# A diffusion-transformer layer on one core: probabilities transposed in squares on VectorE by way of DRAM, partial sums copied back into PSUM, Newton rounds on GpSimd

## The chip, the core and the metric

The kernel runs on one core of one Trainium2 chip. The metric is device time in microseconds (us), the median of several executions. The engines are named TensorE (PE in the profile, its weight loads PEld), VectorE (DVE), ScalarE (ACT), GpSimd (POOL) and SyncE (SP), which here issues all DMAs. SBUF is the on-chip memory, PSUM the banks that TensorE writes. The page of the profile calls buffers by the program's names, with their numbers left out.

## The reference

One layer over 256 latent tokens and 256 context tokens, width 2048, all in fp32:

```python
sh1, sc1, g1, sh2, sc2, g2 = ada_mods(c, w_ada, b_ada)          # from the conditioning vector
qa, ka, va, qb, kb, vb = mixer_qkv(modulate(x, sh1, sc1), w_in, ...)      # 8+8 query heads, 2+2 key heads of 128
...                                                             # the same for the context tokens
heads = concat(window_sink_attention(qa, ka, va, context), global_attention(qb, kb, vb, context))
x = layer_norm(ALPHA * x + g1 * (heads @ w_out), ln1_g, ln1_b)
x = layer_norm(ALPHA * x + g2 * swiglu(modulate(x, sh2, sc2), w_gate, w_up, w_down), ln2_g, ln2_b)
```

Group A has rotary positions, a window and a sink logit per head; group B has RMS-normalised queries and keys (`rms_norm`) and rotary positions. Every latent query sees 256 latent and 256 context keys, so the probabilities of one head for 128 queries are a tile of 128 x 512.

## The kernel before, in words

**Precision.** An fp32 product is made of three passes: each operand is split into a rounded part (`hi`, a cast on ScalarE) and the rest (`lo`, a subtraction on VectorE), and `mm3` (L268 to L271) adds hi x hi, hi x lo and lo x hi in a PSUM bank. A weight piece of 128 x 1024 is cast in L491 and split in L494. Matmuls of plain fp32 (transposes, values) go without a split.

**The first half, up to the first layer norm,** is a list of steps. Each step has an engine, a cost in ns, steps that it must follow, buffers that it takes and gives back, and a due time (`F.at`). The class `Flow` (L67) walks through the list forward and backward in `ROUNDS` rounds, with the costs, the lags between engines (`SAME`, `OTHER`) and the pools, and keeps the order of the round that ends first. The instructions are then issued in that order, and each engine runs its own list strictly in order. So the cost numbers in `F.add` decide the order, not the speed. SyncE's list holds the loads of the weights (1 MB each, in four `raw` and two `araw` buffers) and all other DMAs.

- *Input projection.* The 16 slices of the width are taken in groups of 1, 1, 2, 4 and 8 (`GROUPS`, numbered g = 0 to 4). For each group, the modulated inputs are made (`flow_inputs`), then six blocks of 512 columns (`flow_block`, L646): four query blocks of two row tiles (latent tokens) and two key/value blocks of four row tiles (latent and context). Each row tile takes one of four `acc` banks. At the end of a group the bank is added to a sum in SBUF (`qacc`, `kvacc`) by VectorE (L679), or copied there in group 0.
- *Keys and queries* (`flow_keys`, `flow_queries`): the norm's 1/sqrt comes from squares on ScalarE (L715) and three Newton rounds on VectorE (L287 to L290, `rsqrt_steps`), then rotary multiplications on VectorE, transposes on TensorE, cast and split.
- *Attention* (`flow_attend`, L847): four head groups (gi = 0 to 3) with four pairs each; a pair is two heads for 128 queries, 16 pairs in all. A pair's steps are: scores for both heads (TensorE, banks of the pool `wk`), maximum (VectorE, L873), exponent (ScalarE, L885), inverse of the sum (VectorE), weighing (ScalarE, L898), transposes of the probabilities in four 128 x 128 tiles per head (TensorE, L903), gather of each head's transposed tile from PSUM into `pT` (ScalarE, L908), values (four fp32 matmuls of 256 columns, L914), cast and split of the result (L921, L925).
- *Output projection* (`flow_out`, L1042): per 512 columns, first over early head groups (`first_outs`), whose sums are kept in `outacc`, then over the last ones. VectorE adds bank and sum (L1086), multiplies by the gate (L1089), adds the residual (L1092) and takes statistics (L1098). For the last 512 columns (`by_tile`) the early sum is gated and added ahead (L1089, L1092), so that after the last matmul only the bank's own part is left (L1095).
- Beside this, VectorE sums adaLN vectors (`vector_sum`, L377), and idle time of TensorE at the start is filled with 56 matmuls on the identity (L1124).

**The second half** (FFN, both projections and the second layer norm) is not touched by the change. It transposes its hidden tiles with the way that the change brings to attention: VectorE turns each 32 x 32 square in place and reorders the squares (`squares`, L1367), four DMAs put the result to DRAM so that the rows land in transposed order (`put`, L1372), and one DMA gets it back (`get`, L1377).

Of the kernel before, what the change touches and what calls it, by code (L numbers as in the profile page):

```python
# [22 lines left out]
P = 128  # L23
# [12 lines left out]
NB = 512  # L36
# [17 lines left out]
PUT, GET, PLACE = 6, 8, 9  # L54

# [11 lines left out]
class Flow:  # L67
# [5 lines left out]
    SAME = {"SP": 0, "PE": 0, "ACT": 60, "DVE": 80, "POOL": 80}  # L73
    OTHER = {"SP": 2000, "PE": 270, "ACT": 90, "DVE": 90, "POOL": 150}
# [120 lines left out]
def dit_layer(ctx: ExitStack, tc: tile.TileContext, x, c, cx, c_ctx, w_ada, b_ada, w_in, q_norm_g,  # L195
# [72 lines left out]
    def mm3(ps, xh, xl, w, first, last):  # L268
        nc.tensor.matmul(ps, lhsT=xh, rhs=w[0], start=first, stop=False)  # L269
        nc.tensor.matmul(ps, lhsT=xh, rhs=w[1], start=False, stop=False)  # L270
        nc.tensor.matmul(ps, lhsT=xl, rhs=w[0], start=False, stop=last)  # L271

    def rsqrt_steps(ss, n, done):
# [12 lines left out]
        def newton(i):  # L286
            y, t = st["y"], st["t"]  # L287
            nc.vector.scalar_tensor_tensor(t, y, -0.5, y, op0=ALU.mult, op1=ALU.mult)
            nc.vector.tensor_mul(t, t, ss())
            nc.vector.scalar_tensor_tensor(y, t, 1.5, y, op0=ALU.add, op1=ALU.mult)  # L290
            if i == 2:
                done(y)

        return [first] + [lambda i=i: newton(i) for i in range(3)]

    ea = ExitStack()
# [203 lines left out]

    def flow_products(hl, deps, ready, cols, ps, xs, first, last, prev):

        def fn():
            if first:
                ps.t = acc_bank()
            for i, (c, x) in enumerate(zip(cols, xs)):
                xh, xl = x()
                mm3(ps.t, xh, xl, (hl.hi[:, c : c + NB], hl.lo[:, c : c + NB]),
                    first and i == 0, last and i == len(cols) - 1)
# [3 lines left out]
        return F.add("PE", 681 * len(cols), fn, after, [ps] if first else [], list(hl.rooms))  # L513
# [71 lines left out]
    def flow_part(k0, n, at, each):  # L585
# [17 lines left out]
        for s in range(2):  # L603
# [3 lines left out]
            for j0 in range(0, n, 2):  # L607
# [33 lines left out]
                b = F.add("DVE", 60 + 330 * nj, rest, [a], give=[uf])  # L641
# [4 lines left out]
    def flow_block(g, b, chunks):  # L646
# [7 lines left out]
        ends = {}  # L654
# [19 lines left out]
        for r in rows:  # L674
            dst = qacc[gi][r] if kvi is None else kvacc[kvi][r // 2][:, r % 2, :]

            def evac(dst=dst, ps=accs[r], r=r):
                if g > 0:
                    nc.vector.tensor_add(dst, dst, ps.t)  # L679
                elif r % 2 or b < 2:  # L680
                    nc.vector.tensor_copy(dst, ps.t)
                else:
                    nc.scalar.copy(dst, ps.t)

            eng = "ACT" if g == 0 and not (r % 2 or b < 2) else "DVE"
            evacs[b, r] = F.add(eng, 520 if eng == "ACT" else 710, evac, [ends[r], evacs.get((b, r))], give=[accs[r]])
# [19 lines left out]
    def head_rms(srcs, nh, after, scale=None):  # L706
# [10 lines left out]
        def done(y):  # L717
            if scale is not None:
                f = pa.tile([P, n], F32, tag="qsc", name="qsc", bufs=4)
                nc.vector.tensor_scalar_mul(f, y, scale)  # L720
# [899 lines left out]
```

## Time and profile before

| | |
|---|---|
| median of 3 runs | 1156.09 us (1155.67 to 1156.09) |
| the profiled execution | 1156.38 us, of which 1154.6 us are the span from the first to the last instruction |
| granted TensorE clock, mean | 0.996 |
| instructions in the span | 14326 |
| moved by DMA | 304.49 MB |
| first scores, first transpose after the output projection | at 214.25 us, at 406.15 us of the span |

How to read the lines: busy lines give us, share and count for each engine. A row of a stretch gives each engine's busy us and count, then the granted clock, the share of time that the 16 DMA engines were busy, and GB/s. A group's row is line, engine, operation, written<-read, shape and count, then busy us and mean ns of one, then the idle time just before and what ended it. A row of the chain of waits is start, us, engine, tile and line. A row of the order of time is start, us, engine, line and operation. A DMA row gives the count, KB of each and the median us from issue to landing. The durations of neighbouring instructions of one engine overlap in part.

### The profile page before, as it was taken

The numbers are of one execution on the slowest core, as the hardware profiler recorded it, in microseconds if no ns is written. First come the engines' busy times: TensorE is split into PE (matmuls) and PEld (weight loads), VectorE is DVE, ScalarE is ACT, GpSimd is POOL, SyncE is SP. The second block draws the span as 40 slices with busy tenths as digits, with TensorE's granted clock in tenths as the row PEclk, the third lists the DMA queues.
The fourth block names the chain that finished last, engine by engine and source line by source line (L and its number), as shares of the span: only waits on it lengthen the run. The fifth ranks groups of instructions, "written<-read, shape, count | busy, mean of one in ns | idle before, by whom it ended". The sixth has DMA issues, their size and how long they took to land.

```text
span 1154.6 us, 14326 instructions
## 1 busy us (share of the span) xinstructions
PE 1135.0 (98%) x5475; PEld 919.1 (80%) x5475; DVE 830.9 (72%) x1078; ACT 540.2 (47%) x772; POOL 26.1 (2%) x44
## 2 busy tenths in 40 slices
PE   8999999999999999999999999999999999999995
PEld 8766588888888768888888888888888888888884
DVE  4763489988899988777666666776776787676556
ACT  3331442678776255544464444544544344433341
POOL 1000030000000001000000000000000000000000
PEclk9999999999999999999999999999999999999998
DMA  8999998624588578989967776677677988876641
GB/s 263 382 381 394 396 363 311 221 74 160 185 316 296 175 250 309 349 305 317 312 196 258 224 244 223 225 248 250 227 247 248 323 308 301 315 292 236 208 142 74
DMA packets 166557, 304.49 MB, mean 264 GB/s; under 512 B 7340, under 2 KB 33356, under 8 KB 164183
## 3 DMA queue, kind: packets, MB, share of 16 engines
q1 hardware_dynamic: 166488, 303.58, 75.7%
q8 instruction: 43, 0.70, 0.2%
q14 instruction: 26, 0.21, 0.1%
HBM read 295.68 MB, written 7.86 MB: 263 GB/s over the span
## 4 chain that ended last, share of the span: by engine, by line
PE 94%; DVE 2%; DMA 2%; ACT 1%; issue 0%; SPq 0%; DVEq 0%; ACTq 0%
PE acc L269 27%; PE acc L270 27%; PE acc L271 27%; PE wk L914 2%; PE wk L530 2%; PE acc L1124 1%; PE wk L903 1%; DMA raw<-in_w_in_dram 1%; PE wk L269 1%; PE wk L271 1%; PE wk L270 1%; PE wk L387 1%; PE wk L617 1%; DMA lgb<-in_ln_b_dram 1%; PE wk L967 0%
## 5 line engine op out<-in xcount | busy, mean ns | idle before, releaser
L260 DVE TENSOR_TENSOR lo<-raw,hi 128x1024 fp32r<-128x1024 f32 x258 | 312.5, 1220 | 182.8 <-ACT hi L259 179.3
L259 ACT CAST hi<-raw 128x1024 fp32r<-128x1024 f32 x258 | 271.2, 1055 | 353.4 <-PE acc L271 306.5
L269 PE MATMUL acc<-hi,u2h 128*128 128x512 f32 x704 | 274.6, 390 | 0.2 <-ACT u2h L1443 0.2
L270 PE MATMUL acc<-lo,u2h 128*128 128x512 f32 x704 | 274.0, 389 | 0.7 <-DVE lo L260 0.7
L271 PE MATMUL acc<-hi,u2l 128*128 128x512 f32 x704 | 274.1, 389 | 0.0
L269 PEld LDWEIGHTS acc<-hi,u2h 128*128 128x128 f32 x704 | 132.2, 188 | 28.2 <-ACT u2h L1443 1.1
L270 PEld LDWEIGHTS acc<-lo,u2h 128*128 128x128 f32 x704 | 132.2, 188 | 28.2 <-DVE lo L260 1.1
L271 PEld LDWEIGHTS acc<-hi,u2l 128*128 128x128 f32 x704 | 132.2, 188 | 28.2 <-DVE u2l L1444 0.6
L491 ACT CAST hi<-raw 128x1024 fp32r<-128x1024 f32 (+1 forms) x86 | 87.9, 1033 | 127.2 <-PE acc L271 64.4
L269 PE MATMUL acc<-hi,hTh 128*128 128x512 f32 x344 | 135.5, 394 | 0.0
L271 PE MATMUL acc<-hi,hTl 128*128 128x512 f32 x344 | 133.9, 389 | 0.0
L270 PE MATMUL acc<-lo,hTh 128*128 128x512 f32 x344 | 133.9, 389 | 0.0
L377 DVE SCALAR_TENSOR_TENSOR adav<-raw,cs,adav 128x512 f32<-128x512 f32 (+1 forms) x128 | 121.2, 947 | 9.1 <-DMA raw<-in_w_ada_dram 7.4
L494 DVE TENSOR_TENSOR lo<-raw,hi 128x1024 fp32r<-128x1024 f32 (+1 forms) x86 | 101.8, 1195 | 27.2 <-ACT hi L491 27.0
L269 PE MATMUL acc<-hi,uh 128*128 128x512 f32 x256 | 103.9, 406 | 0.1
L270 PE MATMUL acc<-lo,uh 128*128 128x512 f32 x256 | 100.3, 392 | 0.8 <-DVE lo L494 0.8
L271 PE MATMUL acc<-hi,ul 128*128 128x512 f32 x256 | 100.0, 391 | 0.0
L270 PEld LDWEIGHTS acc<-lo,hTh 128*128 128x128 f32 x344 | 64.6, 188 | 14.4 <-issue 1.0
L269 PEld LDWEIGHTS acc<-hi,hTh 128*128 128x128 f32 x344 | 64.6, 188 | 14.1 <-issue 1.0
L271 PEld LDWEIGHTS acc<-hi,hTl 128*128 128x128 f32 x344 | 64.6, 188 | 13.4
L269 PEld LDWEIGHTS acc<-hi,uh 128*128 128x128 f32 x256 | 48.1, 188 | 15.8 <-issue 5.2
L270 PEld LDWEIGHTS acc<-lo,uh 128*128 128x128 f32 x256 | 48.2, 188 | 10.5 <-DVE lo L494 1.8
(206 smaller groups left out, 1167.5 us busy)
## 6 DMA issues: line engine op xcount, KB each, us to landing
raw<-in_w_ada_dram SPq DMA_DIRECT2D x72, 1024.0 KB, 7.3
raw<-in_w_gate_dram SPq DMA_DIRECT2D x44, 1024.0 KB, 7.3
raw<-in_w_up_dram SPq DMA_DIRECT2D x44, 1024.0 KB, 7.3
raw<-in_w_down_dram SPq DMA_DIRECT2D x44, 1024.0 KB, 5.2
raw<-in_w_ada_dram SPq DMA_DIRECT2D x48, 512.0 KB, 4.5
raw<-in_w_in_dram SPq DMA_DIRECT2D x18, 1024.0 KB, 9.9
raw<-in_w_out_dram SPq DMA_DIRECT2D x16, 1024.0 KB, 5.0
raw<-in_w_in_dram SPq DMA_DIRECT2D x10, 512.0 KB, 6.9
```

The lines of the kernel that those rows point to most:

```text
L259: nc.scalar.copy(hi[:, :n], raw[:, s : s + n])
L260: nc.vector.tensor_tensor(lo[:, :n], raw[:, s : s + n], hi[:, :n].bitcast(F32), op=ALU.subtract)
L269: nc.tensor.matmul(ps, lhsT=xh, rhs=w[0], start=first, stop=False)
L270: nc.tensor.matmul(ps, lhsT=xh, rhs=w[1], start=False, stop=False)
L271: nc.tensor.matmul(ps, lhsT=xl, rhs=w[0], start=False, stop=last)
L377: nc.vector.scalar_tensor_tensor(a[:, c : c + piece], raw[:, f : f + piece], cs[:, 4 * (g * (G4 * NB // w) + j) + 2, None], a[:, c : c + p ...
L387: nc.tensor.matmul(ps, lhsT=ones, rhs=sb[:, s : s + NB], start=True, stop=True)
L491: nc.scalar.copy(hl.hi[:, :n], raw.t[:, s : s + n])
L494: nc.vector.tensor_tensor(hl.lo[:, :n], raw.t[:, s : s + n], hl.hi[:, :n].bitcast(F32), op=ALU.subtract)
L530: nc.tensor.matmul(bank.t[32 * j : 32 * j + 32, :width], lhsT=cs[:, 4 * k + 2 - 2 * i : 4 * k + 34 - 2 * i], rhs=raw.t[:, c * width : (c + ...
L617: nc.tensor.transpose(ps.t[:, (j * 2 + t) * P : (j * 2 + t + 1) * P], src, ident)
L914: nc.tensor.matmul(o_ps.t[:, : 2 * P], lhsT=v, rhs=pT.t[:, k].rearrange("p h q -> p (h q)"), start=k == 0, stop=k == 3)
```

## The change

Three parts, and new costs for the planner:

1. *Probabilities.* Transposes (L903) and gathers (L908) are dropped. VectorE turns a head's 128 x 512 tile in 32 x 32 squares into `hx`; SyncE puts both heads of a pair to DRAM with four DMAs and gets `pT` back with one. The value matmuls now read their 256 columns as eight pieces of 32.
2. *Sums.* In the last group of the input projection (`SEED_G` = 4), and in the output projection where an earlier sum exists, ScalarE copies the sum from SBUF into the bank (`flow_seed`), and the matmuls add to it (no `start`). At the end ScalarE copies the bank out (or VectorE gates it at once). VectorE's adds are dropped there, and the early gating of the last 512 columns with them.
3. *Norms.* The Newton rounds of the head norms, and the scaling behind them, run on GpSimd: four operations a round instead of three, since the combined operation is not used there.
4. The planner's costs and lags are set to other values (examples below), a trip through DRAM is given `SLOW` = 1500 ns more per way, the filler at the start takes a bank of the pool `wk` instead of `acc`, and the DRAM pool is opened earlier.

```diff
+SEED_G = 4
+SLOW = 1500
...
-    SAME = {"SP": 0, "PE": 0, "ACT": 60, "DVE": 80, "POOL": 80}
-    OTHER = {"SP": 2000, "PE": 270, "ACT": 90, "DVE": 90, "POOL": 150}
+    SAME = {"SP": 0, "PE": 0, "ACT": 120, "DVE": 80, "POOL": 80}
+    OTHER = {"SP": 2000, "PE": 270, "ACT": 180, "DVE": 160, "POOL": 150}
...
-            nc.vector.scalar_tensor_tensor(t, y, -0.5, y, op0=ALU.mult, op1=ALU.mult)
-            nc.vector.tensor_mul(t, t, ss())
-            nc.vector.scalar_tensor_tensor(y, t, 1.5, y, op0=ALU.add, op1=ALU.mult)
+            nc.gpsimd.tensor_mul(t, y, y)
+            nc.gpsimd.tensor_mul(t, t, ss())
+            nc.gpsimd.tensor_scalar(t, t, -0.5, 1.5, op0=ALU.mult, op1=ALU.add)
+            nc.gpsimd.tensor_mul(y, y, t)
...
+    def flow_seed(ps, src, after):
+        def fn():
+            ps.t, ps.seeded = acc_bank(), True
+            nc.scalar.copy(ps.t, src())
+        return F.add("ACT", 475, fn, after, [ps])
...
+        ends = {r: flow_seed(accs[r], lambda r=r: sums[r], [evacs[b, r], chunks[0][0][1][0]]) for r in rows} if g >= SEED_G else {}
...
+            eng = "ACT" if g >= SEED_G or g == 0 and not (r % 2 or b < 2) else "DVE"
+            def evac(dst=sums[r], ps=accs[r], eng=eng):
+                if eng == "ACT":
+                    nc.scalar.copy(dst, ps.t)
+                elif g > 0:
                     nc.vector.tensor_add(dst, dst, ps.t)
...
-        for f in rsqrt_steps(lambda: st["ss"], n, done):
-            prev = [F.add("DVE", 720, f, prev)]
+        for i, f in enumerate(rsqrt_steps(lambda: st["ss"], n, done)):
+            prev = [F.add("POOL" if i else "DVE", 1300 if i else 720, f, prev)]
...
-            def flip(i, probs=probs, ps=None):
-                ps.t = wk_bank()
-                for k in range(4):
-                    nc.tensor.transpose(ps.t[:, k * P : (k + 1) * P], probs[i].t[:, k * P : (k + 1) * P], ident)
-            def gather(i, pT=pT, ps=None):
-                if i == 0:
-                    pT.t = b4([P, 4, 2, P], F32, "pT")
-                nc.scalar.copy(pT.t[:, :, i, :], ps.t.rearrange("p (k q) -> p k q", k=4))
+            def squares(i, probs=probs, hx=hx):
+                if i == 0:
+                    hx.t = b4([P, 2, NB], F32, "hx")
+                nc.vector.transpose(hx.t[:, i, :].rearrange("p (r k q) -> p k r q", r=4, k=4),
+                                    probs[i].t.rearrange("p (k r q) -> p k r q", r=4, k=4))
+            def put(hx=hx, st=st):
+                st["hd"] = scratch.tile([4, 32, 2, 4, P], F32, tag="pd", name="pd", bufs=8)
+                for a in range(4):
+                    nc.sync.dma_start(st["hd"][:, :, :, a, :].rearrange("r i h x -> i h r x"),
+                                      hx.t[32 * a : 32 * a + 32].rearrange("i h (r x) -> i h r x", r=4))
+            def get(pT=pT, st=st):
+                pT.t = b4([P, 2, 4, P], F32, "pT")
+                nc.sync.dma_start(pT.t.rearrange("p h a x -> p (h a x)"), st["hd"].rearrange("r i h a x -> (r i) (h a x)"))
...
+                pv = pT.t.rearrange("p h a (k q) -> p k (h a) q", k=4)
                 for k in range(4):
...
-                    nc.tensor.matmul(o_ps.t[:, : 2 * P], lhsT=v, rhs=pT.t[:, k].rearrange("p h q -> p (h q)"),
+                    nc.tensor.matmul(o_ps.t[:, : 2 * P].rearrange("p (g q) -> p g q", q=32), lhsT=v, rhs=pv[:, k],
                                      start=k == 0, stop=k == 3)
...
-            m = [F.add("DVE", 700, lambda i=i, f=largest: f(i), [s[i]]) for i in range(2)]
+            m = [F.add("DVE", 610, lambda i=i, f=largest: f(i), [s[i]]) for i in range(2)]
...
+                g.append(F.add("DVE", 615, lambda i=i, f=squares: f(i), [n[i], *g], [hx] if i == 0 else [], [probs[i]]))
+            a = F.add("SP", 1800, put, g, give=[hx])
+            g = [(F.add("SP", 1300, get, [(a, -SLOW)], [pT]), -SLOW)]
+            v = F.add("PE", 1760, values, g, [o_ps], [pT, *kv_room[w]])
...
+        ends = {t: flow_seed(accs[t], lambda t=t: outacc[n, t], [outs[n, t], first]) for t in range(NT)} if gs[0] else {}
...
-            elif by_tile:
-                at, F.at = F.at, F.at - 6
-                early = steps([outs[n, t], gates[n]], lambda: gate(lambda: outacc[n, t]), base)
-                F.at = at
-                outs[n, t] = steps([ends[t], early], lambda: gate(lambda: ps.t), last, spread, give=[ps])
...
+            a = F.add("DVE", 710, gate, [ends[t], gates[n]], give=[ps])
+            a = F.add("DVE", 710, base, [(a, 80)])
+            outs[n, t] = F.add("DVE", 710, spread, [(a, 80)])
```

More of the change, by code (lines that the diff above doesn't have):

```diff
@@ L508, in fn @@
                 mm3(ps.t, xh, xl, (hl.hi[:, c : c + NB], hl.lo[:, c : c + NB]),
-                    first and i == 0, last and i == len(cols) - 1)
+                    first and not seed and i == 0, last and i == len(cols) - 1, ps.seeded)
         after = [deps[0], (deps[1], 200), ready[0], (ready[1], 400), prev]
-        return F.add("PE", 681 * len(cols), fn, after, [ps] if first else [], list(hl.rooms))
+        return F.add("PE", 688 * len(cols), fn, after, [ps] if first and not seed else [], list(hl.rooms))
     last_load = []
@@ L653, in flow_block @@
         accs = [Buf("acc") for r in rows]
-        ends = {}
+        sums = [qacc[gi][r] if kvi is None else kvacc[kvi][r // 2][:, r % 2, :] for r in rows]
+        ends = {r: flow_seed(accs[r], lambda r=r: sums[r], [evacs[b, r], chunks[0][0][1][0]]) for r in rows} if g >= SEED_G else {}
         done = 0
```

90 lines of the change are left out of this document (34 added, 56 removed).

## The prediction

> **What bounds the kernel now.** I read first the page's busy line and its chain that ended last, then the table of stretches.
>
> ```profile
> PE 1135.0 (98%) x5475; PEld 919.1 (80%) x5475; DVE 830.9 (72%) x1078; ACT 540.2 (47%) x772; POOL 26.1 (2%) x44
> PE 94%; DVE 2%; DMA 2%; ACT 1%; issue 0%; SPq 0%; DVEq 0%; ACTq 0%
> ...
> core 0: us, PE busy (x) PEld busy (x) DVE busy (x) ACT busy (x) POOL busy (x), PEclk, DMA share, GB/s
> 0.00:200.00 200.00, 195.89 (x1193) 147.51 (x1194) 125.83 (x170) 70.50 (x105) 14.08 (x25) 1.00 0.98 356
> 200.00:406.00 206.00, 206.00 (x1020) 166.80 (x1018) 184.48 (x327) 133.26 (x275) 1.77 (x4) 1.00 0.59 204
> 440.00:1133.00 693.00, 692.27 (x3079) 572.60 (x3078) 474.09 (x499) 313.66 (x348) 9.26 (x14) 1.00 0.76 259
> ```
>
> The chain is TensorE for 94% of the span, at full granted clock. Up to 200 us it shares the bound with DMA (share 0.98). From 200 to 406 us, where attention and the output projection lie and where nearly the whole change acts, TensorE has no gap and DMA is busy only 0.59 of the time. After that the code is the same. So an instruction less on TensorE in the second stretch is worth its full time, as long as nothing else arrives later. VectorE is the nearest competitor (184.5 of 206 us). DMA is very unevenly used there:
>
> ```profile
> 240.00:260.00 20.00, 20.00 (x103) 15.91 (x102) 16.98 (x47) 14.67 (x43) 0.00 (x0) 1.00 0.33 106
> 320.00:340.00 20.00, 20.00 (x98) 16.77 (x98) 18.79 (x25) 13.41 (x27) 0.00 (x0) 1.00 0.90 316
> ```
>
> **The change part by part.** *1. TensorE loses the transposes of the probabilities.* In order of time, the chain shows a group of four and its neighbours:
>
> ```profile
> 223.00 0.44 PE wk L903 x4
> 358.73 0.87 PE wk L903 x8
> 357.00 1.73 PE wk L914 x8
> 359.60 0.23 PE acc L269
> L903 PE MATMUL wk<-ident,pr 128*128 128x128 f32 x128 | 18.4, 272 | 0.0
> ```
>
> The 272 ns of one overlap with its neighbours; the chain's 0.44 us for four is what the engine's stream is longer by. There are 128 / 4 = 32 groups: 32 x 0.44 = **14.1 us** off. The order of the changed program, from the first score matmul to the first transpose after the output projection, has the same 604 matmuls of 512 columns and 64 value matmuls (0.23 and 0.43 us), but 48 transposes where there were 176; TensorE gets nothing new.
>
> *2. In their place: VectorE squares, ScalarE loses the gathers, SyncE gains 80 DMAs.*
>
> ```profile
> L1367 DVE STREAM_TRANSPOSE spill<-spill 128x512 f32<-128x512 f32 x20 | 13.0, 685 | 0.0
> L908 ACT COPY pT<-wk 128x512 f32<-128x512 f32 x32 | 18.5, 595 | 4.4 <-PE wk L903 4.0
> L679 DVE TENSOR_TENSOR qacc<-qacc,acc 128x512 f32<-128x512 f32 x6 | 4.1, 680 | 0.6 <-PE acc L271 0.6
> L679 DVE TENSOR_TENSOR kvacc<-kvacc,acc 128x512 f32<-128x512 f32 x4 | 2.6, 681 | 0.5 <-PE acc L271 0.5
> L1086 DVE TENSOR_TENSOR oacc<-oacc,acc 128x512 f32<-128x512 f32 x8 | 5.4, 679 | 0.3 <-PE acc L271 0.2
> L1080 ACT COPY oacc<-acc 128x512 f32<-128x512 f32 x8 | 4.8, 595 | 1.3 <-PE acc L271 1.3
> L288 DVE SCALAR_TENSOR_TENSOR rs_t<-rs_y 128x8 f32<-128x8 f32 x9 | 1.4, 156 | 0.0
> 252.86 1.28 DVE L873 TENSOR_REDUCE m<-wk 128x1 f32<-128x512 f32 x2
> ```
>
> VectorE gains 32 x 0.685 = 21.9 us. It loses 16 adds of the last group of the input projection (10.9), 8 adds of the output projection (5.4), two early gates and two early adds (2.8), and 29 Newton instructions (29 x 0.156 = 4.5). The net is -1.7 us, but only ten of the 16 adds lay behind 200 us (the two L679 rows are of that stretch), so there it is about +2.4: 187 busy of 192 us. Durations overlap (two reductions take 1.28, not 1.37), so at the pace of 0.60 for 512 elements the stretch is some 90 to 94% full. ScalarE loses 32 gathers and gains 26 seeds and 18 copies out: +12 x 0.595 = 7.1 us on 133. Both stay under TensorE; I cost them at nothing. The seeds need cover: a bank's next use now waits for copy out and copy in (1.19 us) instead of one add (0.68). Behind a key/value block three other rows are still to run, 3 x 6 x 0.23 = 4.1 us, and a query block takes two of four banks. Without that cover 18 seeds in the input and output sums would cost up to 0.5 us each, 9 us.
>
> *3. The added wait: values wait for a trip through DRAM.* Each of the 16 pairs of heads now goes squares, four puts of 128 KB, one get of 512 KB, values. The nearest rows are the same trip at half size, in the FFN:
>
> ```profile
> hd<-spill SPq DMA_DIRECT2D x80, 64.0 KB, 4.3
> spill<-hd SPq DMA_DIRECT2D x20, 256.0 KB, 5.3
> L1372 SPq DMA_DIRECT2D hd<-hx x8: 430/438/660, 901.9 to 910.7; - x8
> DMA to landing us min/median/max: 1.6/4.5/7.1
> DMA to landing us min/median/max: 5.6/6.4/7.1
> raw<-in_w_ada_dram SPq DMA_DIRECT2D x12, 1024.0 KB, 5.0
> raw<-in_w_ada_dram SPq DMA_DIRECT2D x16, 512.0 KB, 4.5
> ```
>
> The first landing line is that of the tile hd (all its puts and gets), the second that of hx (eight puts at the busiest time); the last two rows are of the stretch from 200 to 406 us. The last put leaves 3 x 0.44 = 1.3 us after the first, lands 4.3 later, and the get takes 5.3: 10.9 us. For the doubled size I add 0.5, which is what 512 KB more cost the loads of this stretch: **11.4 us**. Below, two landings of 1.6 plus the issue make 4.5; above, 1.3 + 7.1 + 7.1 = 15.5.
>
> How long may it take? In the new order the tightest pair is the sixth. From its scores to its values TensorE has 63 matmuls of 512 (14.5), two other pairs' values (3.5) and eight transposes (0.9): 18.8 us. VectorE, in its order from that pair's last reduction to its second square, has three reductions and four squares (7 x 0.61), two splits of a weight piece (2 x 1.14), two half tiles (2 x 0.34) and six small ones (6 x 0.19): 8.4, with about 0.2 for the start. That leaves 10.2, and 9.8 when what VectorE is still behind with is carried along. The others, counted alike, have 10.2 to 15.7 (pairs 14, 15, 16: 10.2, 11.2, 10.7). A trip of 11.4 is late by 1.6 at pair 6; pairs 7 and 8 are under way and move along. It is late again by 1.2 at pair 14, which carries 15 and 16. **TensorE waits 2.8 us.** SyncE's queue is in order too: behind a put that waits for its squares stand weight loads. The order has one or two between the puts of two pairs, each load has one of four buffers, and up to 300 us DMA has room, so I cost this at nothing beyond the 2.8.
>
> From the ninth get to the sixteenth it has none: 13 loads of 1 MB, 28 puts and 7 gets, 21 MB, are in the queue between them, and TensorE's work between these values is 28 x 0.43 + 166 x 0.23 = 50 us. The most that DMA moves in this trace is
>
> ```profile
> 100.00:120.00 20.00, 20.00 (x104) 13.97 (x106) 6.58 (x9) 1.99 (x2) 0.00 (x0) 1.00 1.05 405
> ```
>
> so 21 MB want 52 us. I take this as inside the 1.2 at pair 14; it is the first place to look if I am wrong.
>
> *4. Newton rounds on GpSimd.* 36 dependent operations, between 279 and 944 ns each by the rows below, 12 per norm: 3.3 to 11.3 us. The first norm has 5 us of VectorE work between its start and its user; the others much more. Cost nothing; 6 us at worst.
>
> ```profile
> L960 POOL TENSOR_TENSOR mA<-lcol,sc 128x4 f32<-128x4 f32 x4 | 3.8, 944 | 286.7 <-DVE sc L975 286.7
> L962 POOL TENSOR_TENSOR mB<-mB,sh 128x4 f32<-128x4 f32 x4 | 1.1, 279 | 0.3
> ```
>
> *5. The order.* The planner's costs change too, and with them the lists of all engines. Ahead of the first scores TensorE's list has the same instructions, and SyncE's differs by a few exchanged loads. DMA is full there, and TensorE has one gap:
>
> ```profile
> 120.00:140.00 20.00, 19.15 (x119) 11.93 (x112) 8.65 (x12) 11.19 (x18) 0.00 (x0) 1.00 1.04 393
> ```
>
> An exchanged load of 1 MB can close that gap of 0.85 or open another like it. I take nothing, and 1 us to both sides.
>
> *Sum.* The profiled execution took 1156.38 us, 1154.6 of span and 1.8 around it: 1156.4 - 14.1 + 2.8 = 1145.1. It lies 0.3 above the median of the three runs, so I forecast **1144.8**.
>
> **The rivals.** *A. No wait at all: 1142.0.* Where DMA share is 0.33, as around pair 6, a landing is nearer the 1.6 than the 4.3; the trip is then 5 to 9 us, under every room. Against it speak pairs 14 to 16. The Trainium skill, page "DMA: Bandwidth & Descriptors", section "Anatomy of one DMA", has, for DMAs that GpSimd issues, 2.0 us fixed plus bytes at 436 GB/s: an estimated 8.1 us for this trip and so this case; no run before shows an idle trip, and the FFN's 4.3 and 5.3 are longer.
>
> *B. VectorE becomes the bound: about 1150.* If the 187 us are nearer to 97% than to 92% of 192, in-order waits of 5 us more are likely. GpSimd may add to it: while it built tables, two VectorE operations ran 0.36 and 0.12 us long.
>
> ```profile
> 163.69 1.64 DVE L377 SCALAR_TENSOR_TENSOR g1b<-raw,cs,g1b 128x1024 f32<-128x1024 f32 x1 [2.90 <-DMA raw<-in_w_ada_dram]
> 165.26 1.34 DVE L494 TENSOR_TENSOR lo<-raw,hi 128x1024 fp32r<-128x1024 f32 x1
> L377 DVE SCALAR_TENSOR_TENSOR g1b<-raw,cs,g1b 128x1024 f32<-128x1024 f32 x17 | 21.7, 1277 | 0.2 <-DMA raw<-in_w_ada_dram 0.2
> ```
>
> At half a microsecond for each of 38 operations a full block costs 19 us of VectorE, some 5 beyond its slack: 1150 again. The Trainium skill, page "SBUF — State Buffer", section "SBUF: two separate sides", has this as an exclusive lock on a shared port pair; by the row above the loss was partial.
>
> *C. The trip is late everywhere: 1162, slower.* At the FFN's busiest time puts land in 6.4; with 7.1 for the get the trip is 1.3 + 6.4 + 7.1 = 14.8. Scores to values is about 21 us of a stretch of 137, so lateness is paid about 6.5 times; 14.8 exceeds the rooms by 3 on average: 6.5 x 3 = 19.5, 1156.4 - 14.1 + 19.5 = 1161.8. It decides from 14.1 / 6.5 = 2.2 average lateness, a trip of about 14 us. For it: the 21 MB in 50 us. Against: the 5.0 that 1 MB loads take in this stretch.
>
> *D. Values get slower: up to 1170.* Their moving operand now comes in eight pieces of 32 columns. Doubled, 16 x 1.73 = 27.7 is lost; half as long again already eats the gain. No row has such a matmul; on VectorE, pieces of 32 cost what a plain tile costs:
>
> ```profile
> L741 DVE TENSOR_TENSOR qrot<-qacc,sinQ 128x256 f32<-128x256 f32 x4 | 1.7, 416 | 0.0
> L788 DVE TENSOR_TENSOR kTl<-wk,kTh 128x256 fp32r<-128x256 f32 x8 | 3.1, 416 | 1.7 <-ACT kTh L785 1.7
> ```
>
> **How the numbers follow.** Forecast (1142.5 to 1149) 60%; A 12%; B 10%; C 14%, of which 4 end within 0.2% of before; D 4%. 0.2%, 2.3 us, is about what a measurement of this kernel can tell from none. So faster 82%, same 4%, slower 14%. From 1141 to 1156 some 15% is left out above (C, D) and 5% below (the far side of A, and a start that gains from its new order).
>
> **What would show it.** Right: the values' group unchanged at 1.73 us; no transposes of probabilities on TensorE; the first transpose after the output projection near 395 us instead of 406; TensorE's waits in the stretch named to a get of pT, 2 to 4 us, at the sixth and the last three pairs; get landings near 5; no difference after 440 us but the shift. Wrong: TensorE waiting at most pairs for pT (C); VectorE without idle time and TensorE waiting for its splits (B); values above 2 us (D); a later arrival at the first scores (214 us now), which would put the loss into the start, where I assume no change.

## The result, and the profile after

The changed kernel takes **1165.39 us** (median of 4 executions, 1164.05 to 1168.93) against 1156.09 of the kernel before on the same chip: ratio **1.0083**, 95% interval 1.0059 to 1.0108. It is slower by 0.8%; the forecast was 1144.8 and faster. The profiled execution is the longest of the four (1168.93, span 1167.2).

The page of the changed kernel, first the busy time of each engine, then the shares of the chain that ended last:

```profile
PE 1130.9 (97%) x5347; PEld 912.2 (78%) x5347; DVE 829.0 (71%) x1053; ACT 546.9 (47%) x784; POOL 36.8 (3%) x82
...
PE 78%; DMA 9%; DVE 9%; issue 2%; ACT 1%; SPq 1%; DVEq 0%; ACTq 0%
```

TensorE has 128 instructions less, as forecast, but 4 us less of busy time, not 14; part of its work ran at a lower clock, as shown below. And the chain, which was TensorE for 94%, is TensorE for 78%: DMA and VectorE have come into it with 9% each.

The table of stretches of the changed kernel (the stretch of the change now ends at 413.3, where the first transpose after the output projection starts):

```profile
0.00:200.00 200.00, 194.26 (x1170) 146.40 (x1171) 121.73 (x163) 78.45 (x120) 14.88 (x25) 0.98 0.96 353
200.00:413.30 213.30, 201.59 (x923) 159.08 (x921) 186.72 (x309) 131.58 (x272) 13.37 (x42) 0.99 0.84 278
450.00:1145.00 695.00, 692.69 (x3074) 572.67 (x3073) 475.08 (x499) 314.16 (x348) 7.56 (x14) 1.00 0.76 258
80.00:100.00 20.00, 19.86 (x86) 16.98 (x87) 10.53 (x16) 10.21 (x17) 0.00 (x0) 0.83 0.92 340
240.00:260.00 20.00, 18.18 (x88) 14.59 (x88) 17.39 (x41) 12.06 (x38) 3.37 (x13) 1.00 0.75 232
320.00:340.00 20.00, 16.83 (x74) 13.43 (x72) 13.96 (x21) 10.15 (x18) 0.00 (x0) 1.00 0.99 310
360.00:380.00 20.00, 18.18 (x68) 13.91 (x69) 15.23 (x17) 6.15 (x11) 0.00 (x0) 0.91 1.00 340
```

Three things are new. TensorE has gaps in attention: 11.7 us of 213.3, where before it had none. VectorE, which should have been busier, is *less* busy in the worst rows (14.0 of 20 us at 320 and 15.2 at 360, where it had 18.8 and 19.8), so it waits too. And the granted clock, 1.00 in every such row before, is 0.83 at 80 us and 0.91 at 360. DMA share at 240 went from 0.33 to 0.75 and at 320 from 0.90 to 0.99.

I divide both profiled spans at two places. From the first score matmul to the first transpose after the projection I call the *middle*.

| us | to the first scores | middle | the rest | span |
|---|---|---|---|---|
| before | 213.3 | 192.7 | 748.5 | 1154.6 |
| changed | 218.4 | 194.9 | 753.9 | 1167.2 |
| forecast | 213.3 | 181.4 | 748.5 | 1143.3 |

So the gain of 11.3 in the middle became a loss of 2.2, and the two parts in which I expected no difference lost 5.1 and 5.4.

Two reservations. These are single executions: five kernels below (gets_gpsimd, no_wait, no_wait_gp, no_trip and after_late5) have the same lists up to the first scores, and in their profiles these come at 213.7 to 217.7 us. So a part of the 5.1 belongs to this one execution. And eight small matmuls (L1267, which sum adaLN vectors on TensorE) lie in the middle in the changed kernel and in the rest before. They are about 0.9 us, since the 32 of the middle are busy for 3.6.

*The middle.* What TensorE waited for there (us in all, times, longest):

```profile
PE wk L939 <- DMA pT<-pd: 8.5, 5, 3.0
PE acc L273 <- DVE oTl L950: 1.6, 1, 1.6
PE wk L939 <- ACT pr L901: 1.6, 1, 1.6
```

The groups of the same stretch (the new squares, the values, one of the Newton operations), and its DMAs:

```profile
L921 DVE STREAM_TRANSPOSE hx<-pr 128x512 f32<-128x512 f32 x32 | 22.4, 703 | 0.1
L939 PE MATMUL wk<-pT,kvacc 128*128 128x256 f32 x128 | 32.4, 398 | 10.1 <-DMA pT<-pd 8.5 <-ACT pr L901 1.6
L290 POOL TENSOR_TENSOR rs_t<-rs_y 128x8 f32<-128x8 f32 x9 | 4.1, 450 | 94.9 <-DVE rs_y L285 94.5
```

```profile
pd<-hx SPq DMA_DIRECT2D x64, 128.0 KB, 5.7
pT<-pd SPq DMA_DIRECT2D x16, 512.0 KB, 4.0
raw<-in_w_ada_dram SPq DMA_DIRECT2D x16, 512.0 KB, 6.7
```

Each operation costs about what I took for it: squares 0.70 (0.685 taken), puts 5.7 (4.3), gets 4.0 (5.3); the last two are medians of the 12 puts and 10 gets whose landing the trace has. What goes wrong shows in SyncE's list. Its order of time around the sixth to the eighth pair, then the squares of the seventh and eighth, then the sixth pair's values:

```profile
273.33 2.81 SPq L927 DMA_DIRECT2D pd<-hx  x4
281.13 0.33 SPq L932 DMA_DIRECT2D pT<-pd  x1
281.50 2.57 SPq L927 DMA_DIRECT2D pd<-hx  x4
286.66 0.33 SPq L932 DMA_DIRECT2D pT<-pd  x1
287.09 0.39 SPq L473 DMA_DIRECT2D raw<-in_w_out_dram  x1
287.52 2.94 SPq L927 DMA_DIRECT2D pd<-hx  x4
295.43 0.33 SPq L932 DMA_DIRECT2D pT<-pd  x1
```

```profile
278.99 0.71 DVE L921 STREAM_TRANSPOSE hx<-pr 128x512 f32<-128x512 f32 x1
285.18 0.70 DVE L921 STREAM_TRANSPOSE hx<-pr 128x512 f32<-128x512 f32 x1
```

```profile
285.05 1.99 PE L939 MATMUL wk<-pT,kvacc 128*128 128x256 f32 x8 [0.73 <-DMA pT<-pd]
```

The sixth pair's trip is undisturbed: puts at 273.33, get at 281.13, values at 285.05, 11.7 us in all (I had 11.4). But between the last put (276.14) and the get, 5.0 us, SyncE issues nothing: it stands before the get until the puts have landed. The seventh pair's squares are done at 279.70 and their puts leave at 281.50, the eighth's at 285.88 and 287.52. Over the 16 pairs the puts leave 1.6 to 6.1 us late nine times, and a weight load that stands between them is as late. What SyncE, and then VectorE, waited for from 210 to 400 us:

```profile
SPq L932 <- DMA pd<-hx: 54.3, 26, 4.9
SPq L473 <- DVE lo L498: 16.7, 5, 7.7
```

The second of these rows in the kernel before, where a weight load is L469:

```profile
SPq L469 <- DVE lo L494: 100.7, 16, 19.0
```

And VectorE in the changed kernel:

```profile
DVE adav L381 <- DMA raw<-in_w_ada_dram: 5.5, 2, 2.8
DVE g1b L381 <- DMA raw<-in_w_ada_dram: 3.6, 2, 2.7
```

SyncE lost 54.3 us before gets; its slack, the waits for a free weight buffer, has shrunk from 100.7 to 16.7. The adaLN loads come late, VectorE stands 9.1 us before their sums, and what is behind these sums in its list (squares, maxima) stands with it.

*The rest.* The second row tile's norm in VectorE's order of time, in the changed kernel and before:

```profile
417.94 0.75 DVE L381 SCALAR_TENSOR_TENSOR adav<-raw,cs,adav 128x512 f32<-128x512 f32 x1
418.80 0.74 DVE L381 SCALAR_TENSOR_TENSOR adav<-raw,cs,adav 128x512 f32<-128x512 f32 x1
419.58 0.75 DVE L381 SCALAR_TENSOR_TENSOR adav<-raw,cs,adav 128x512 f32<-128x512 f32 x1
420.43 0.74 DVE L381 SCALAR_TENSOR_TENSOR adav<-raw,cs,adav 128x512 f32<-128x512 f32 x1
421.33 0.55 DVE L1065 TENSOR_SCALAR xt<-xt,mv,ly 128x512 f32<-128x512 f32 x1
```

```profile
411.53 0.75 DVE L377 SCALAR_TENSOR_TENSOR adav<-raw,cs,adav 128x512 f32<-128x512 f32 x1
412.32 0.74 DVE L377 SCALAR_TENSOR_TENSOR adav<-raw,cs,adav 128x512 f32<-128x512 f32 x1
412.98 0.54 DVE L1040 TENSOR_SCALAR xt<-xt,mv,ly 128x512 f32<-128x512 f32 x1
413.44 1.53 DVE L377 SCALAR_TENSOR_TENSOR adav<-raw,cs,adav 128x512 f32<-128x512 f32 x2
```

No line of this code is changed, but its order is: four sums instead of two stand ahead of the normalisation, and TensorE waits 2.49 us for it instead of 1.36. In the FFN a wait for a weight split grew from 0.73 to 2.31 in the same way.

*The clock.* Around that wait, in stretches of 1 us of the changed kernel:

```profile
420.00:421.00 1.00, 0.00 (x0) 0.00 (x0) 1.00 (x3) 0.00 (x0) 0.00 (x0) 1.00 1.06 412
422.00:423.00 1.00, 0.98 (x5) 1.00 (x6) 0.00 (x0) 0.28 (x1) 0.00 (x0) 0.50 0.80 145
426.00:427.00 1.00, 0.98 (x7) 0.55 (x6) 0.59 (x3) 0.00 (x0) 0.52 (x1) 1.00 0.00 0
```

After the gap TensorE is granted 0.50 for 3.4 us, which costs 1.7. This happened four times: at 80 us (6.8 us long, after a gap of 1.7), 360, 422 and 613: 8.5 us lost, on top of the gaps.

### The profile page after: what moved, and what is told of

Same layout as the page of the kernel before. It is cut to its first block, busy times and chain, and to the rows that moved or that the text cites. A ratio compares the mean times of both kernels' runs of the same rounds, so it can differ in the third digit from the quotient of the medians.

```text
span 1167.2 us, 14247 instructions
## 1 busy us (share of the span) xinstructions
PE 1130.9 (97%) x5347; PEld 912.2 (78%) x5347; DVE 829.0 (71%) x1053; ACT 546.9 (47%) x784; POOL 36.8 (3%) x82
## 4 chain that ended last, share of the span: by engine, by line
PE 78%; DMA 9%; DVE 9%; issue 2%; ACT 1%; SPq 1%; DVEq 0%; ACTq 0%
PE acc L271 24%; PE acc L273 24%; PE acc L272 24%; DMA raw<-in_w_ada_dram 5%; PE wk L546 2%; DVE lo L498 2%; DMA pd<-hx 2%; PE wk L1130 1%; DVE g1b L381 1%; DMA pT<-pd 1%; SPq L927 1%; PE wk L939 1%; DVE hx L921 1%; DMA raw<-in_w_in_dram 1%; DVE adav L381 1%
## 5 line engine op out<-in xcount | busy, mean ns | idle before, releaser
L271 PEld LDWEIGHTS acc<-hi,hTh 128*128 128x128 f32 x344 | 64.6, 188 | 14.1 <-issue 0.7
```

## The experiments

Theory M: the trip costs in two ways at once, by TensorE's wait for pT and by SyncE's wait for the puts, which makes the loads late. Rivals were the trip's length alone (T), VectorE's load (V), and order and clock outside the trip (S, then O). The expectations are quoted as written; Q is M's part for SyncE's queue. Milestones in them are counted from the first score matmul or the mask behind it, 0.7 to 1 us apart.

### Where the middle went: the changed kernel's lists, one wait taken away at a time

In these four, TensorE's, VectorE's and ScalarE's lists are those of the changed kernel, so the middle holds the same work in all.

**gets_gpsimd**

```diff
-                nc.sync.dma_start(pT.t.rearrange("p h a x -> p (h a x)"), st["hd"].rearrange(...))
+                nc.gpsimd.dma_start(pT.t.rearrange("p h a x -> p (h a x)"), st["hd"].rearrange(...))
```

> The changed kernel with one edit: the 16 gets of pT are issued by GpSimd instead of SyncE; the lists of TensorE, VectorE and ScalarE are the same to the letter. Theory Q (SyncE's queue): in the changed kernel a get stands 5 us in SyncE's list until its puts have landed, and the next pair's puts (late by 1.6 to 6 us at 9 of 16 pairs) and weight loads stand behind it. Then TensorE's waits named to pT fall from 8.5 to 3 us or less, puts leave within 0.5 us of their squares, the first transpose after the output projection comes at 404 to 408 us instead of 413.3, and the whole takes 1156 to 1161. Theory T (the trip itself is too long for the room that scores to values leaves): the waits for pT stay at 7 to 9 us and the time within 2 us of the changed kernel. Theory S (start and clock, nothing to do with the trip): the first scores stay at 219 us in any case.

Measured 1165.44, ratio 1.0080 (1.0056 to 1.0104): no gain. The puts do leave at their squares, VectorE's wait for adaLN loads falls to 0.3 us. But a get by GpSimd lands in 5.9 us instead of 4.0, and TensorE's waits for pT stay:

```profile
PE wk L939 <- DMA pT<-pd: 9.7, 6, 3.0
```

So Q alone, as I had put it, fails: the queue is not the only wait. What the queue alone is worth this run can't tell exactly, since its gets land later.

**no_wait**

```diff
-                pv = pT.t.rearrange("p h a (k q) -> p k (h a) q", k=4)
+                pv = xt[:, 0, : 2 * NB].rearrange("p (g k q) -> p k g q", k=4, q=32)
```

> The changed kernel with the value matmuls reading a slice of xt of the same shape instead of pT (the result of attention is left out; squares, puts and gets are all still made, and every engine's list is unchanged). It shows what the trip costs by its wait alone. Theories Q and T: waits for pT (8.5 us) go, and the half clock at 360 us with them (1.8): first transpose after the output projection near 403 us, total 1153 to 1157. If instead VectorE or DMA is the bound behind the wait, other waits take their place and the total stays at 1161 or more.

Measured 1164.71, ratio 1.0076 (1.0053 to 1.0099): no gain either, against both Q and T. Without a wait for pT, TensorE and VectorE waited so:

```profile
PE wk L939 <- ACT pr L901: 5.8, 1, 5.8
PE acc L273 <- DVE oTl L950: 4.0, 1, 4.0
```

```profile
DVE adav L381 <- DMA raw<-in_w_ada_dram: 12.4, 3, 5.5
SPq L932 <- DMA pd<-hx: 54.5, 27, 5.7
```

The late loads now end the same idle time: VectorE stands 12.4 us before its adaLN sums, and TensorE behind VectorE.

**no_wait_gp** and **no_trip**: the first is both edits above; the second is no_wait with `put` and `get` doing nothing.

> no_wait and gets_gpsimd together: values read a slice of xt (the result of attention is left out), all puts and gets are made, the gets by GpSimd, so that SyncE's queue never stands behind a put's landing and TensorE never behind a get. Only the trip's bytes and its 64 puts in SyncE's queue are left. Theory Mq (the queue makes the loads late, 54 us of SyncE's time waiting for puts): 178 to 182 us from the first scores to the first transpose after the projection. Theory Mb (the trip's bytes, DMA share 1.0 from 300 to 400 us): 187 us or more with VectorE still waiting for adaLN loads. Theory V: 188 or more with VectorE's waits near nothing.

> The changed kernel with values reading a slice of xt (as in no_wait; the result of attention is left out) and without the 64 puts and 16 gets: no trip, no DMA of it, nothing of it in SyncE's queue; TensorE's, VectorE's and ScalarE's lists are unchanged. From the first scores to the first transpose after the output projection the kernel before takes 192.1 us, the changed one 194.0, no_wait 192.8; the 14.1 us of transposes are missing in the last two, so a TensorE without waits would take 178. Theory M (the trip loads DMA and SyncE's queue, the adaLN and weight loads behind it come late, and VectorE stands in order behind them): 178 to 181 us, whole 1146 to 1151. Theory V (VectorE with its squares is the bound): 188 us or more, whole 1159 or more.

Measured 1153.99 for no_wait_gp, ratio 0.9988 (0.9972 to 1.0004), and 1148.54 for no_trip, ratio 0.9934 (0.9919 to 0.9949). Stretches of no_trip:

```profile
240.00:260.00 20.00, 20.00 (x96) 16.04 (x95) 19.21 (x44) 14.67 (x44) 3.15 (x13) 1.00 0.25 85
320.00:340.00 20.00, 20.00 (x91) 16.73 (x90) 18.16 (x29) 16.29 (x31) 0.00 (x0) 1.00 0.68 248
```

| us | middle, profiled execution | saved against the changed kernel | median of the whole |
|---|---|---|---|
| changed | 194.9 | | 1165.39 |
| get not in SyncE's queue (gets_gpsimd) | 191.9 | 3.0 | 1165.44 |
| no wait for pT (no_wait) | 193.5 | 1.4 | 1164.71 |
| both (no_wait_gp) | 182.1 | 12.8 | 1153.99 |
| no trip at all (no_trip) | 179.9 | 15.0 | 1148.54 |

Either wait removed alone gives 1 to 3 us of the middle and under 1 us of the whole; both give 12.8 and 11.4. The trip's bytes and the puts' own issue add 2.2 in these profiles (5.5 by the medians, with executions of no_wait_gp from 1150.1 to 1159.4). So the bytes, a part of the 21 MB that I had named as the first place to look, are not the main loss. M holds, and V falls: with every square still on VectorE (19.2 of 20 us at 240) TensorE waits 0.7 us in the whole middle of no_trip, and 179.9 is within 1.3 of 192.7 - 14.1. VectorE is close behind, though: it is busy for 171.2 of these 179.9 us.

### The planner's numbers for the trip

**true_costs**

```diff
-            a = F.add("SP", 1800, put, g, give=[hx])
-            g = [(F.add("SP", 1300, get, [(a, -SLOW)], [pT]), -SLOW)]
+            a = F.add("SP", 2800, put, g, give=[hx])
+            g = [(F.add("SP", 400, get, [(a, -5000)], [pT]), -2200)]
```

> The changed kernel with the planner's numbers for the trip set to what the trace shows: puts 2800 ns of SyncE instead of 1800, puts to get 5.0 us later instead of 3.5, the get 400 instead of 1300, get to values 4.2 instead of 3.5. No instruction is added or removed, only the order. Theory Q: the planner puts other loads and puts between a pair's puts and its get and other matmuls ahead of the values; waits for pT at 3 us or less, total 1152 to 1160. Theory T: there is no other work to put there, the waits go to another cause (VectorE, loads), total 1163 or more. Theory S: the first scores move only if SyncE's list ahead of them moves.

Measured 1155.87, ratio 0.9998 (0.9984 to 1.0012): 9.5 us less than the changed kernel, by order alone. SyncE's wait before gets, 54.3 us before:

```profile
SPq L932 <- DMA pd<-hx: 5.8, 9, 1.6
```

In SyncE's list a load or the next pair's puts now stand between a pair's puts and its get. Around the sixth and seventh pair:

```profile
274.19 6.84 SPq L927 DMA_DIRECT2D pd<-hx  x8
281.13 0.56 SPq L473 DMA_DIRECT2D raw<-in_w_out_dram  x1
281.86 0.43 SPq L932 DMA_DIRECT2D pT<-pd  x1
```

TensorE's waits for pT are 1.1 us, and the middle is 187.9, with work in it that is about 1.8 us more (18 matmuls of 512 columns and four transposes more, 24 of the small ones of L1267 fewer). With the planner's 1.8 us for four puts (the trace has 2.8) and 3.5 to the get (5.0) it had believed the queue free.

### The parts alone

**flips_back** is the changed kernel with L903 and L908 of before in place of squares, put and get. **seeds_only**, **newton_only** and **costs_only** are the kernel before with part 2, part 3 or part 4 alone (of part 4 what applies without a trip).

> The changed kernel without part 1: the probabilities are transposed on TensorE and gathered by ScalarE as before; seeds, Newton rounds on GpSimd and the planner's numbers stay as changed. Theory S: the new numbers alone bring the gap of 1.55 us at 78 us and the half clock behind it; first scores at 218 to 220 us, total 1158 to 1163. Theory Q or T alone: first scores at 214, total 1154 to 1157.

> The kernel before with part 2 alone (sums copied back into PSUM), the planner's old numbers. In its VectorE list two of the four adaLN sums stand between the second row tile's norm and its transposes, as before; in the changed kernel and all runs so far four do. Theory O (the order that follows the change in code that it does not touch costs 2 to 7 us after 406 us): TensorE's wait at the second tile's transposes stays at 1.4 us, that in the FFN near 0.7, no half clock, whole 1153 to 1158. Against O: waits of 2 us at these two places all the same, and 1159 or more. If seeds lack cover, the time up to 406 us grows by up to 9 us with waits named to ScalarE's copies.

> The kernel before with part 3 alone: Newton rounds on GpSimd, the planner's old numbers. If GpSimd costs nothing in attention, as I took it: first scores at 213 to 214, 192 to 193 us to the first transpose, and only the sums ahead of the second tile's transposes cost 1 to 4 us: 1156 to 1160. If GpSimd slows VectorE, its squares, splits and reductions are longer than in the kernel before by 0.1 us or more between 220 and 280 us, and attention takes 195 us or more.

> The kernel before with part 4 alone: the planner's new costs and lags, and the filler in a bank of the other pool; no instruction of the stages is another. If the planner's numbers bring the loss at the start and the new order behind the projection, flips_back's 1162.8 is found here: first scores at 215 us or later, a wait of 2 us or more at the second tile's transposes (four sums stand ahead of them in VectorE's list here too), 1159 to 1163. If they do not, first scores at 213 to 214 and 1156 to 1158, the 1 us of the two more sums being all.

The middles of these hold slightly different work, since each has an order of its own ahead of the scores.

| | median us | ratio, 95% | middle | waits at second transposes, FFN |
|---|---|---|---|---|
| flips_back | 1162.77 | 1.0055 (1.0037 to 1.0073) | 192.4 | 1.97, 1.8 |
| seeds_only | 1156.86 | 1.0002 (0.9993 to 1.0012) | 194.0 | 0.8, 0.6 |
| newton_only | 1156.74 | 1.0005 (0.9996 to 1.0015) | 190.8 | 1.45, 1.6 |
| costs_only | 1157.77 | 1.0018 (1.0008 to 1.0029) | 189.7 | 1.22, 1.6 |

Alone, seeds and Newton rounds change nothing that can be measured, and the planner's numbers cost 0.2%. The time of flips_back lies in S's range, but its first scores come at 214.8 us, not at 218 to 220: the early loss of the changed kernel is not found there. It is found in the profile of seeds_only, the longest of its ten executions: a gap of 1.73 us at 78 us, with half clock behind it. seeds_only is the one kernel whose VectorE list kept its order behind the projection, and its two waits are the smallest, as O says. But costs_only and newton_only have four sums ahead of the normalisation and wait only 1.2 to 1.5, so the count of sums is not the whole of it. The three parts together (flips_back) lose 6.5 us, more than their sum of about 3. Its five executions, 1159.3 to 1165.5 us, have mean granted clocks of 0.996 falling to 0.991: 0.005 of 1160 is 5.8 us, so the clock can make up nearly all of the spread between them. Why this combination is granted less is not settled.

### The order behind the projection

**late5** is true_costs with the edit below; **before_late5**, **after_late5** and **flips_late5** are the kernel before, the changed one and flips_back with it.

```diff
-    run(first_half[2:3])
-    run(merge(first_half[3 : 2 * ONE_F], scales))
+    run(first_half[2:5])
+    run(merge(first_half[5 : 2 * ONE_F], scales))
```

> true_costs with one more edit, in the second half: the adaLN sums that stood ahead of the second row tile's transposes are issued two steps later, so none of the four stands there. Theory O: the 2.5 us wait at these transposes falls to 0.5 or less and with it the chance of a half clock (3.4 us in the profile of true_costs); whole 1149 to 1154, with a narrower spread than the 1153.5 to 1159.2 of true_costs. Against O: the time stays within 1 us of true_costs' 1155.9.

> The kernel before with the one edit of late5 (the adaLN sums of the second half two steps later). It tells how much of late5's gain has nothing to do with the change. Theory O: TensorE's wait at the second row tile's transposes falls from 1.36 us to 0.3 or less, nothing else moves much: 1154.5 to 1156. If the edit itself brings more (loads, FFN order), 1153 or less.

> The changed kernel with the one edit of late5 and the planner's numbers as changed. Theory O: the wait of 2.5 us at the second tile's transposes falls under 0.5, the half clock behind it goes, the part from the first transpose on falls from 753.9 to about 749 us; the waits in attention stay, so 1158 to 1162 instead of 1165.4. If the time stays at 1164 or more, the order at that place was not what costs.

> flips_back (transposes on TensorE, no trip, seeds and Newton rounds on GpSimd) with the one edit of late5. It prices part 1 once the rest is mended: late5, with part 1 and true planner numbers, took 1150.5. From flips_back's profile: 214.8 to the first scores, 192.4 to the first transpose, 750.2 after it; with the wait there gone 748.5 to 749: 1156 to 1159 as median. If it comes to 1151 or less, part 1 brings nothing even with the planner's true numbers.

TensorE's wait at the second transposes in late5:

```profile
407.69 0.63 PE L1300 MATMUL wk<-ident,xt 128*128 128x128 f32 x4 [0.32 <-DVE xt L1065]
```

| | without the edit | with it | ratio to before, with it |
|---|---|---|---|
| before | 1156.05 | 1155.91 | 1.0000 (0.9991 to 1.0009) |
| changed | 1165.39 | 1160.03 | 1.0032 (1.0021 to 1.0044) |
| flips_back | 1162.77 | 1158.02 | 1.0015 (1.0006 to 1.0023) |
| true_costs | 1155.87 | **1150.53** | 0.9957 (0.9941 to 0.9973) |

The edit is worth nothing where the wait was 1.36 and the clock stayed full, and about 5 us in each kernel that had a wait of 2 to 2.5 there. It takes away more than this wait: the one for a weight split in the FFN falls too, from 2.1 us in true_costs to 0.8 in late5. Between these two profiles the rest is shorter by 6.3 us (755.7 and 749.4); the first wait makes up 2.2, the second 1.3, and the half clock behind the first 3.4. So O holds, for the two waits and the clock together; they are not told apart by time. late5 beats both kernels. And flips_late5 against late5 prices part 1 with the order that comes with it, once planned truly: 7.5 us of the 14.1.

### What goes with part 1

**late5_gp** is late5 with the gets by GpSimd, **late5_dve** late5 with the Newton rounds back on VectorE, **squares_late5** the kernel before with part 1, the true trip numbers and the later sums, but neither part 2 nor 3.

> late5 with the 16 gets issued by GpSimd, every other engine's list unchanged. Theory Mq as no_wait against no_wait_gp showed it (193.5 to 182.1 us when SyncE no longer stands behind the puts): attention takes 182 to 185 us instead of 186.4, whole 1147 to 1149. Against it: gets by GpSimd landed in 5.9 us instead of 4.0, so TensorE waits longer for pT and the whole stays at 1150 to 1153.

> late5 with the Newton rounds back on VectorE (29 operations of 0.15 us, 4.5 us of VectorE). If VectorE is near its bound in attention: 1152 to 1155, attention 188 us or more instead of 186.4. If not: 1150 to 1151, within the spread of late5.

> The kernel before with part 1 alone (probabilities by squares and the trip), the true planner numbers for the trip, and the sums of the second half later as in late5. Against before_late5's 1155.9: the transposes give 14.1 us, waits of 5 to 8 us come back as in late5 (6.3 from 192.7 to 186.4). VectorE has its adds and Newton rounds still, some 17 us more than in late5: if it is near its bound, 1152 to 1158; if it is not, 1149 to 1151 and parts 2 and 3 are worth nothing beside part 1.

late5_gp took 1150.46, ratio 0.9958 (0.9944 to 0.9972): as late5, and not the 1147 to 1149 of Mq. Once SyncE's queue is planned with its true times, moving the gets off it buys nothing. late5_dve took **1148.33**, ratio 0.9935 (0.9918 to 0.9951), the fastest of all and below both ranges that I had given. Its middle (186.7) is that of late5 (186.4), so Newton rounds on GpSimd buy nothing there; the kernel with them is 2.2 us slower, though its order is another one too. The first scores of late5_dve come 4.5 us earlier: ahead of them TensorE is busy for 203.3 us instead of 205.3, and idle for 4.9 instead of 7.4. Its rest is 2.1 us longer, with the last eight of those small matmuls in it (0.9). What in the order makes the waits is not settled. squares_late5 took 1173.86, ratio 1.0150 (1.0135 to 1.0165), far outside what I expected. Its middle, 205.8 us, in one row, and TensorE's longest waits in it:

```profile
215.00:420.00 205.00, 186.78 (x823) 145.76 (x825) 183.53 (x335) 109.86 (x219) 0.52 (x1) 0.97 0.78 267
```

```profile
PE wk L923 <- ACT pr L887: 10.1, 3, 4.4
PE acc L271 <- DVE lo L496: 4.4, 1, 4.4
```

TensorE waits for banks that an exponent still has to read and for a weight split, not for the trip: no row there names pT. VectorE is busy 183.5 us in this middle; in that of late5_dve 173.3 of 187, so it is not fuller (90% and 93%). TensorE stands for 18.2 us of this row, and half clock behind four of its gaps costs 6.8 more. Part 1 without part 2 is thus far from a gain, though part 2 alone is worth nothing. The VectorE adds that part 2 takes away may be behind it, but no run shows that: this kernel also has the planner's other numbers as before, and the two are not told apart.

## Why the prediction was wrong, step by step

1. *TensorE loses 14.1 us*: right. With no trip to wait for, the middle fell by 12.8.
2. *VectorE and ScalarE stay under TensorE, seeds are covered*: right in the changed kernel (squares 0.703 us; TensorE waits 0.7 us in the middle of no_trip with all of them; seeds_only no difference).
3. *The trip, 2.8 us of waiting*: **the step that failed.** Its length was right: 11.4 forecast, 11.7 measured at pair 6 (8.3 to 13.6, median 11.7, at the ten pairs where the trace has the get's landing). What failed is the sentence that SyncE's queue costs nothing beyond it. I priced the get as a DMA that takes 5.3 us to land, not as an instruction that holds SyncE's list for the 5.0 us until the puts have landed: 54.3 us in all, for 16 pairs. Behind it stood the next pair's puts, and loads on which VectorE waited. I also took 0.44 us to issue a put, where SyncE needs 0.62 in the median and 2.6 to 4.1 for four. TensorE waited 8.5 us for pT, not 2.8, and at pairs 3, 6, 8, 11 and 14 instead of the sixth and the last three; 3.2 more went to an exponent and a split of a result that came late, and 1.7 to the half clock behind one of these waits. With the planner told of the queue, true_costs has 1.1 us of waits for pT and is 9.5 us faster.
4. *Newton rounds cost nothing*: right for the part alone (newton_only took 1156.74); beside part 1, with the order that they bring, late5 is 2.2 us slower than late5_dve. GpSimd did not lengthen VectorE's operations: splits were 1213 ns and reductions 680 (1218 and 684 before). Rival B's way over the port is not seen on VectorE; GpSimd's own operations went from 0.20 to as much as 1.20 us. The exclusive lock that the Trainium skill has (page "SBUF — State Buffer", section "SBUF: two separate sides") would show here, if at all, as a delay of GpSimd.
5. *The order, 1 us to both sides, and the same code after 440 us*: wrong. The order of the unchanged second half is worked out anew as well. It brought two waits of 2.3 to 2.5 us where there had been 1.36 and 0.73, with 1.7 us of half clock behind each; one edit of that order took about 5 us back. Ahead of the scores a gap of 1.7 us came at 78 us, and the half clock behind it cost 3.4 us. This one is in part chance: in the five other profiles with the same lists up to there the gap is 0.95 us or less and the clock full.
6. *The clock* had no term at all. In the trace of before it was 1.00 in every row I read; the longest gap of TensorE there, from 20 us on, was 1.36 us. In the changed kernel it took 8.5 us. The profiled execution lost 12.6 in all: TensorE was idle for 36.3 us of the span instead of 19.6, which is 16.7 more, half clock took 8.5, and the transposes gave 14.1 back; 1.5 of the 12.6 is not assigned.

With steps 3 and 5 mended, late5 takes 1150.5 and late5_dve 1148.3, still 5.7 and 3.5 us above the forecast: in late5 TensorE is idle for 7.4 us ahead of the first scores and 4.1 in the middle, before it was 4.1 and nothing.

Of the rivals, C (trip late everywhere, 1162) had the right sign and nearly the size, but by luck, since its cause is not the one: no_wait takes its wait away and the time stays. D did not happen: the median value matmul took 379 ns before and after, and a group 1.54 to 1.82 us where the clock was full (1.54 to 1.78 before). That the get landed in 4.0 us, under my 5.3, did not help: the wait before it was the price.

## What to carry to other kernels

Where a change puts a dependent pair of DMAs into a queue that is issued in order, price the second one by the time it holds the queue until the first has landed, and list what stands behind it; then let the planner know that time. When one wait is removed and nothing is gained, remove it together with the next suspect before dropping either: here each alone was worth 1 to 3 us, both 13. And price a gap of 2 us on TensorE at more than its length: here about half of those of 2.0 to 2.6 us cost 1.7 or 3.4 us on top. That holds wherever it falls, also in code that the edit does not touch but whose order is worked out anew.

## What the runs showed of the hardware

**The clock after a gap.** All gaps of TensorE of 1 us or more between 20 and 1135 us, over the profiles of both kernels and the 16 experiments:

| gap, us | gaps | with granted clock 0.50 behind them |
|---|---|---|
| 1.0 to 1.5 | 19 | 1 (and one that runs on into a longer gap) |
| 1.5 to 2.0 | 21 | 4 |
| 2.0 to 2.6 | 15 | 8 |
| over 2.6 | 11 | 9 |

Each stretch of half clock behind them was 3.4 or 6.8 us long, a loss of 1.7 or 3.4 us. A gap of 2.49 us was followed by one in the changed kernel and not in gets_gpsimd. The Trainium skill, page "TensorE: Matmul & The Clock Gate", section "Part 1: The HAM clock gate (the "warmup" mystery)", has a free-running window of about 3.4 us, which agrees with these lengths and with the same gap being punished in one kernel and not in another. It has the clock fall after an idle window of that length; here gaps of 1.3 (once) to 3.0 us were enough.

**Gets by GpSimd** of 512 KB landed in 5.9 us (median of 16), by SyncE in 4.0 (of the 10 whose landing the trace has), in the same order of everything else; no_wait_gp against no_wait has 6.2 and 4.2.
